# Load order, high-half casts and sample gating in a hybrid attention and recurrence layer

## The chip, the cores and the metric

The kernel runs on one core of a Trainium2 chip as one launch. The metric is the device time of an execution in microseconds (us), measured several times; beside the times there is one execution recorded by the profiler, from which all durations come. Engines: PE (TensorE; PEld is its loading of weights), DVE (VectorE), ACT (ScalarE), POOL (GpSimd) and SP (SyncE), which in this kernel issues every transfer (DMA).

## The reference

One step of a one-layer encoder, for a prompt of 2048 tokens and for 8 running samples of 16 new tokens each:

```python
proj = jnp.einsum('btd,de->bte', x, w_in)                 # D = 1024 -> 8 sections of 512
qa, ka, va, ga, qh, fh, ih, gh = jnp.split(proj, idx, axis=-1)

# A) stick-breaking attention, 8 heads x 64; samples see 1024 cached keys and values as well
z = jnp.einsum('bhqd,bhkd->bhqk', qblk, kf) * scale
log_keep = jnp.where(mask, jax.nn.log_sigmoid(-z), 0.0)
later = lax.cumsum(log_keep, axis=3, reverse=True) - log_keep
w = jnp.where(mask, jnp.exp(jax.nn.log_sigmoid(z) + later), 0.0)
o_sb = jnp.einsum('bhqk,bhkd->bhqd', w, vf) * jax.nn.silu(ga)

# B) HGRN2 recurrence, 4 heads x 128, chunk by chunk: S_t = diag(f_t) S_{t-1} + k_t outer i_t, o_t = S_t^T q_t
o_hg = rms_norm(o_hg) * norm_g * jax.nn.silu(gh)

out = jnp.einsum('bte,ed->btd', jnp.concatenate([o_sb, o_hg], -1), w_out)
y = layer_norm(alpha * x + out, ln_g, ln_b)
```

The keys, values and the recurrence's last states are outputs too.

## The kernel before

Matrix products of the projections are made in three passes, with each factor split into a high half (rounded to a short form) and a low half (the rest): `split(hi_engine, lo_engine, ...)` writes both, the high one by the helper of line 109 (ACT, a cast) or 111 (POOL), the low one as a difference in line 117. The program has these stages, by the profile's times:

- 0 to about 1010 us: the input projection, in two halves of tokens, section by section in tiles of 384 or 256 tokens. `pe_T` (L309-315) and `pe_N` (L323-325) make the products, `evac_T` (L336-367) and `evac_N` take them out of PSUM. For queries and keys of the prompt `evac_T` copies with ACT into `ev` (L352), splits with POOL into `e2` (high half L111, low half L117) and stores to `qT_d` or `kT_d` in device memory (L362); of gates it makes a SiLU into `ev` (L333) and stores to `gT_d` (L358). The weights' low halves `wl` are POOL's too (L117). The recurrence of the heads (`hgrn`, L405-540) is woven in as chains: intra-chunk scores `ps` (L430-469) from `hq` and `kS` (DVE, L455-456), outputs `on` (DVE, L518) and `qz` (POOL, L532).
- about 1010 to 1600 us: attention of the prompt, in units of one query block by up to 512 keys. `z_part` makes scores z from `kst` and `qr` (L742, L744); the sigmoids are ACT's (L747, L750); `s_part` scans the products of what is kept (DVE, L711) and multiplies them into the weights s (POOL, L764); `t_part` transposes these to wt (PE, L777); `c_part` multiplies with the values `vst` (L795); `finish` gates by `gt` into `mo` and stores a pair of blocks to `mx_d` (L800-815).
- woven into it until about 1353 us, as a guest whose pieces are taken at a set rate: the samples. `sample_init` (L818-842) makes the new tokens' own scores, sends them through device memory (`zn_d`, L836) and reads them back as `snc` (eight loads, L841), after which POOL masks them (L842). Then come rounds, two per sample (keys 512 to 1023, then 0 to 511): `sample_k` transposes cached keys `kr` (L877) and makes scores, `sample_r` scans, `sample_v` turns the weights and multiplies with cached values `vr` (36 matmuls, L958, in four runs with other work between), `sample_o` copies the result to `om` (ACT, L969), transposes it to `pse` (L973) and gates it into `ms_` (DVE, L978). `pk`, `zs`, `so` and `pse` share two PSUM buffers, in turn.
- until 1749 us: the output projection and the LayerNorm, the second guest.

What sets the order: the attention advances in steps of two halves. `at(step, fn)` puts loads at a step (L719-730; a step before the first is taken as the first, that is -12, before the attention itself). `later` holds work for the next half step. `defer(fn, n)` puts a transfer at the end of one list; each `tick()`, once in a half step, counts all entries down and issues from the front those that have come to zero, so that an entry is never issued ahead of one put there earlier. All transfers are then issued by SP, in the order of the program: one that waits for its data or its buffer holds all behind it. `load_k`, `load_v` and `load_q` (L170-193) fetch keys, values and queries of the prompt, `load_g` (L713) a gate, `load_ks` (L845) and `load_vs` (L853) cached keys (1 MB each, two buffers) and values (0.5 MB each, four buffers).

## Time and profile before

| | us |
|---|---|
| median of 3 runs | 1758.91 (1754.67 to 1759.86) |
| the profiled execution, whole | 1750.87 |
| its span, first to last instruction | 1749.1 |
| mean granted TensorE clock (1 is full speed) | 0.990 |

The page gives busy times of each engine; an engine's busy time is that of its instructions, without register, semaphore and transfer-issuing ones. A wait is the idle time of an engine just ahead of an instruction, put down to what released it last. In rows of groups stand the line, engine and operation, output<-input with shape, the count, then busy us and mean ns of one, then the idle time ahead and its releasers. In the rows of the timeline stand the start, the duration, the engine and line, and in brackets the idle time before with its releaser; xN means N instructions in one row. Buffer numbers are left out of names.

### The profile page before, as it was taken

Reading aid. Unit: us, or ns where it says so; the run is one execution under the profiler, and the core shown is the slowest. Engines: PE = TensorE matmul, PEld = TensorE weight load, DVE = VectorE, ACT = ScalarE, POOL = GpSimd, SP = SyncE. Lnnn points to the kernel's source line nnn. Section 1 sums busy time; section 2 is a strip of 40 time slices with the busy share of each in tenths; the row PEclk is TensorE's granted clock in tenths of the full one; section 3 lists DMA queues with packets and bytes.
Section 4 is the critical chain, followed back from the end, with each engine's and each line's share of the span. In section 5 each row is a group of like instructions: output and inputs, shape, how many; then the busy total and the mean of one; then the engine's idle time right before and its main releaser. Section 6 shows DMA issues by size and latency. Waiting matters only on the chain.

```text
span 1749.1 us, 33560 instructions
## 1 busy us (share of the span) xinstructions
PE 1673.7 (96%) x12901; PEld 1517.1 (87%) x12901; DVE 978.7 (56%) x1762; ACT 688.9 (39%) x1593; POOL 830.6 (47%) x918
## 2 busy tenths in 40 slices
PE   8999999999989999999999979999999999999998
PEld 8999999999979999999999957777777777778886
DVE  4264543255544263641746347787878786666554
ACT  3221220212213121221122147777878997775110
POOL 1252323232552151331324546676767876665664
PEclk9999999999999999999999988999999999999999
DMA  5133132122345133231212397989895764431443
GB/s 162 56 114 102 62 95 79 44 73 63 95 127 166 37 112 83 67 111 43 73 51 90 111 224 157 212 180 212 175 220 126 224 166 112 105 88 57 134 147 116
DMA packets 298792, 204.13 MB, mean 117 GB/s; under 512 B 113533, under 2 KB 275849, under 8 KB 298633
## 3 DMA queue, kind: packets, MB, share of 16 engines
q1 hardware_dynamic: 298632, 201.98, 43.9%
q8 instruction: 103, 1.69, 0.4%
q14 instruction: 57, 0.46, 0.1%
HBM read 146.36 MB, written 56.10 MB: 116 GB/s over the span
## 4 chain that ended last, share of the span: by engine, by line
PE 82%; DVE 6%; ACT 4%; DMA 3%; issue 2%; POOL 1%; SPq 1%; POOLq 0%; DVEq 0%; ACTq 0%
PE pj L313 10%; PE pj L315 10%; PE pj L314 10%; PE po L795 7%; PE z L742 5%; PE wt L777 5%; PE pj L323 4%; PE ps L430 4%; PE py L1125 4%; PE pj L325 4%; PE pj L324 4%; PE py L1127 4%; PE py L1126 4%; DMA qr<-qT_d 1%; DVE kS L456 1%
## 5 line engine op out<-in xcount | busy, mean ns | idle before, releaser
L313 PE MATMUL pj<-xh,wh 128*128 128x384 f32 (+1 forms) x1152 | 396.1, 344 | 0.0
L764 POOL TENSOR_TENSOR s<-s,pr 128x512 f32<-128x512 f32 (+3 forms) x320 | 324.9, 1022 | 121.8 <-DVE pr L711 103.8
L315 PE MATMUL pj<-xh,wl 128*128 128x384 f32 (+1 forms) x1152 | 376.6, 327 | 0.0
L314 PE MATMUL pj<-xl,wh 128*128 128x384 f32 (+1 forms) x1152 | 376.3, 327 | 0.0
L117 POOL TENSOR_TENSOR wl<-wr,wh 128x512 fp32r<-128x512 f32 x126 | 164.8, 1331 | 383.6 <-ACT wh L109 383.5
L711 DVE TENSOR_TENSOR_SCAN pr<-keep,pr,one 128x513 f32<-128x513 f32 x192 | 238.4, 1270 | 47.8 <-ACT keep L750 36.7
L313 PEld LDWEIGHTS pj<-xh,wh 128*128 128x128 f32 x1152 | 217.9, 189 | 2.7 <-issue 0.7
L314 PEld LDWEIGHTS pj<-xl,wh 128*128 128x128 f32 x1152 | 218.1, 189 | 0.7 <-issue 0.7
L315 PEld LDWEIGHTS pj<-xh,wl 128*128 128x128 f32 x1152 | 217.3, 189 | 0.0
L742 PE MATMUL z<-kst,qr 128*128 128x512 f32 (+3 forms) x640 | 186.2, 401 | 21.5 <-DMA qr<-qT_d 12.6
L109 ACT COPY wh<-wt 128x512 f32<-128x512 f32 (+3 forms) x320 | 165.0, 548 | 87.4 <-PE wt L777 85.8
L747 ACT ACTIVATE s<-z 128x512 f32<-128x512 f32 (+3 forms) x320 | 183.1, 572 | 19.4 <-PE z L744 15.6
L777 PE MATMUL wt<-ident,s 128*128 128x128 f32 x1088 | 166.3, 281 | 2.1 <-POOL s L764 1.9
L323 PE MATMUL pj<-wh,xh 128*128 128x256 f32 x544 | 160.6, 295 | 0.0
L777 PEld LDWEIGHTS wt<-ident,s 128*128 128x128 f32 x1088 | 123.8, 142 | 35.9 <-issue 16.3
L324 PE MATMUL pj<-wl,xh 128*128 128x256 f32 x544 | 152.6, 281 | 0.1
L325 PE MATMUL pj<-wh,xl 128*128 128x256 f32 x544 | 152.5, 280 | 0.0
L742 PEld LDWEIGHTS z<-kst,qr 128*128 128x128 f32 x640 | 105.1, 195 | 43.5 <-ACT keep L750 18.8
L795 PEld LDWEIGHTS po<-wh,vst 128*64 128x64 f32 x2176 | 118.0, 137 | 26.2 <-issue 18.0
L111 POOL TENSOR_SCALAR e<-ev 128x384 fp32r<-128x384 f32 (+1 forms) x48 | 53.1, 1106 | 178.6 <-ACT ev L352 159.2
L795 PE MATMUL po<-wh,vst 128*64 128x128 f32 x2176 | 137.3, 277 | 0.0
L750 ACT ACTIVATE keep<-z 128x512 f32<-128x512 f32 (+2 forms) x230 | 133.7, 581 | 0.0
(164 smaller groups left out, 2936.5 us busy)
## 6 DMA issues: line engine op xcount, KB each, us to landing
wr<-in_w_in SPq DMA_DIRECT2D x64, 512.0 KB
qr<-qT_d SPq DMA_DIRECT2D x64, 256.0 KB
kr<-in_cache_k SPq DMA_DIRECT2D x16, 1024.0 KB
vr<-in_cache_v SPq DMA_DIRECT2D x32, 512.0 KB
kst<-kT_d SPq DMA_DIRECT2D x24, 512.0 KB
mt<-mx_d SPq DMA_DIRECT2D x136, 64.0 KB
x<-in_x_prompt SPq DMA_DIRECT2D x16, 512.0 KB
out<-xr SPq DMA_DIRECT2D x16, 512.0 KB
```

Of the source, the lines that this page charges most:

```text
L313: mm(o, wh[:, k], xh[:, k, :n], start=k == 0, stop=False)
L314: mm(o, wh[:, k], xl[:, k, :n], start=False, stop=False)
L315: mm(o, wl[:, k], xh[:, k, :n], start=False, stop=k == KT - 1)
L323: mm(o, xh[:, k, ts], wh[:, k], start=k == 0, stop=False)
L324: mm(o, xh[:, k, ts], wl[:, k], start=False, stop=False)
L325: mm(o, xl[:, k, ts], wh[:, k], start=False, stop=k == KT - 1)
L711: dve.tensor_tensor_scan(pr[:, CW - wd:CW + 1][:, ::-1], kr, by, carry, ALU.mult, ALU.bypass)
L742: mm(z[:, :wd], q[:, a, r, q0:q0 + P], k[:, a, k0:k0 + wd], start=r == 0, stop=r == 1 and not top)
L747: act.activation(s[:, :wd], z[:, :wd], AF.Sigmoid, scale=SC)
L764: pool.tensor_tensor(s[:, :wd], s[:, :wd], pr[:, CW - wd + 1:CW + 1], ALU.mult)
L777: nc.tensor.transpose(pt_[:, x:x + P], U[(u, a)][0][:, x:x + P], ident)
L795: mm(o[r], v[:, lo // P % 8 + x, r], th[a][:, x * P:(x + 1) * P], start=top and x == 0, stop=bot and x == n - 1, skip_group_check=True)
```

## The change

Four things are edited.

1. `evac_T`: the high half of prompt queries and keys is made by ACT instead of POOL (48 tiles, 32 of 384 tokens and 16 of 256), `e2` has two buffers instead of one, `ev` two instead of three, and the store is deferred four ticks instead of three.
2. Loads of the first attention job (the loop of L719-730): the second query group is loaded at the very start instead of four steps before its use; the second pieces of keys and values and the gates, which were loaded at the start, come at steps of their own.
3. Stores of `mo` are deferred six ticks instead of four. `load_ks` in `sample_k` is deferred two ticks. `sample_v` makes its 36 matmuls in one run and then defers all four loads of the next sample's values by three ticks, where it issued each load between the runs.
4. `sample_o` keeps the copies `om` of four samples (five buffers) and then makes the four transposes into one PSUM tile and the gate in eight DVE instructions, where every sample had one transpose and two. At the end eight ticks instead of four empty the list.

```diff
             elif sec == GH:
                 silu_to(hg["g"][:, t0:t0 + n], o, n, ng[:, j:j + 1])
             else:
-                e = ev.tile([P, TW], F32, name="ev", tag="ev", bufs=3)
+                e = ev.tile([P, TW], F32, name="ev", tag="ev", bufs=2)
                 if sec == GA:
                     silu_to(e[:, :n], o, n)
                 else:
                     act.copy(e[:, :n], o)
                 if sec != GA:
-                    e2 = ev.tile([P, 2, TW], F32R, name="e2", tag="e2", bufs=1)
+                    e2 = ev.tile([P, 2, TW], F32R, name="e2", tag="e2", bufs=2)
                 for a, c, m in spans(half, t0, n):
                     if sec == GA or c == T:
                         d = gT_d[j][:, c:c + m] if sec == GA else (qn_d if sec == QA else kn_d)[j]
                         defer(lambda d=d, a=a, m=m: dma.dma_start(d, e[:, a:a + m]))
                         continue
-                    split(pool, pool, e2[:, 0, :m], e2[:, 1, :m], e[:, :m])
+                    split(act, pool, e2[:, 0, :m], e2[:, 1, :m], e[:, :m])
                     d = (qT_d if sec == QA else kT_d)[j]
                     defer(lambda d=d, c=c, m=m: dma.dma_start(d[:, :, c:c + m].rearrange("s p t -> p s t"),
-                                                              f32(e2[:, :, :m])), 3)
+                                                              f32(e2[:, :, :m])), 4)
                 if sec == KA:
                     return (half, j, t0, n, e)
...
             order_c = list(chunks(job))[::1 if b0 == 0 else -1]
             for i, c in enumerate(order_c):
                 if job or c:
-                    at((n0 - 5, n0 + 1 if b0 == 0 else n0 - 2)[i] if job else -99, lambda j=job, c=c: load_k(j, c))
-                at((n0, first[job] + (3 if b0 == 0 else 0))[i] if job else -99, lambda j=job, c=c: load_v(j, c))
+                    at((n0 - 5, n0 + 1 if b0 == 0 else n0 - 2)[i], lambda j=job, c=c: load_k(j, c))
+                at((n0 if job else -99, first[job] + (3 if b0 == 0 else 0))[i], lambda j=job, c=c: load_v(j, c))
             for g in range(b0 // 4, b1 // 4):
                 n1 = first[(p, g)] - LZ
                 if job or g:
-                    at(n1 - 4, lambda p=p, g=g: load_q(p, g))
-                at(n1 + GO if job else -99, lambda p=p, g=g: load_g(p, g))
+                    at(n1 - 4 if job or g > 1 else -99, lambda p=p, g=g: load_q(p, g))
+                at(n1 + GO, lambda p=p, g=g: load_g(p, g))
         def z_part(u):
             if u >= NU or u < 0:
...
                 done.add((p, qb // 2))
             if e:
-                defer(store, 4)
+                defer(store, 6)
         def sample_init():
...
                 pool.memset(sn, 0.0)
                 pool.tensor_copy(sn[:, cs], snc[:, b])
                 rows[b] = sn
-            load_ks(*((b, 0) if c == 1 else (b + 1, 1)))
+            defer(lambda: load_ks(*((b, 0) if c == 1 else (b + 1, 1))), 2)
             kr = kraws.pop((b, c))
             ks_ = []
             for p in range(4):
...
                 for p in range(4):
                     r = slice(32 * p, 32 * p + 32)
                     mm(o[r], t[:, r], v(p), start=n == 0, stop=n == len(blocks) - 1)
-                if n in (2, 4, 6):
-                    if b + 1 < NB:
-                        load_vs(b + 1, 1 if n < 6 else 0, (n // 2 - 1) % 2)
-                    yield
             if b + 1 < NB:
-                load_vs(b + 1, 0, 1)
-            yield
+                for c in (1, 0):
+                    for jh in range(2):
+                        defer(lambda c=c, jh=jh: load_vs(b + 1, c, jh), 3)
+            yield
+
+        oms = []
         def sample_o(b):
-            om = sk.tile([P, P], F32, name="om", tag="om")
+            om = sk.tile([P, P], F32, name="om", tag="om", bufs=5)
             act.copy(om, so.pop(b))
-            yield
-            yield
-            pse = px.tile([P, 4, 2, TS], F32, name="pse", tag="px")
-            nc.tensor.transpose(pse.rearrange("q p a t -> q (p a t)"), om, ident)
+            oms.append(om)
+            if len(oms) < 4:
+                return
+            yield
+            yield
+            b0 = b - 3
+            pse = px.tile([P, 4, 4, 2, TS], F32, name="pse", tag="px")
+            for i in range(4):
+                nc.tensor.transpose(pse[:, i].rearrange("q p a t -> q (p a t)"), oms[i], ident)
+            oms.clear()
             def gate():
                 for a in range(2):
                     r = slice(a * DH, (a + 1) * DH)
-                    dve.tensor_tensor(ms_[r, :, b * TS:(b + 1) * TS], pse[r, :, a],
-                                      gs[r, :, b * TS:(b + 1) * TS], ALU.mult)
+                    v = lambda t: t[r, :, b0 * TS:(b0 + 4) * TS].rearrange("d p (b t) -> d b p t", t=TS)
+                    for i in range(4):
+                        dve.tensor_tensor(v(ms_)[:, i], pse[r, i, :, a], v(gs)[:, i], ALU.mult)
             later.append(gate)
             yield
...
         run_later()
         run_later()
         run_later()
-        for _ in range(4):
+        for _ in range(8):
             tick()
         for _ in guest:
             run_later()
```

How instructions stand. First SP's transfers from the first load of values in the attention on, before the change (`kst`, `vst`, `qr`, `gt`: keys, values, queries, gates of the prompt; `qs`, `ks`, `vs`, `gs`: the samples' new tokens; `kr`, `vr`: cached keys and values; `mx_d`: the store of `mo`):

```order
L185 DMA vst<-v_d 128x8x128
L178 DMA kst<-kT_d 64x2x512 x2
L185 DMA vst<-v_d 128x4x128
L716 DMA gt<-gT_d 128x512 x3
L192 DMA qr<-qT_d 64x2x512 x4
L819 DMA qs<-qn_d 128x4x128
L820 DMA ks<-kn_d 128x4x128
L850 DMA kr<-in_cache_k 128x32x64
L823 DMA vs<-vs_d 128x512
L824 DMA gs<-gT_d 128x4x128
L836 DMA zn_d<-ss 128x512 x2
L841 DMA snc<-zn_d 16x8x16 x8
```

The same queue from the same load on, after the change:

```order
L185 DMA vst<-v_d 128x8x128
L192 DMA qr<-qT_d 64x2x512 x4
L178 DMA kst<-kT_d 64x2x512 x2
L716 DMA gt<-gT_d 128x512
L819 DMA qs<-qn_d 128x4x128
L820 DMA ks<-kn_d 128x4x128
L716 DMA gt<-gT_d 128x512
L850 DMA kr<-in_cache_k 128x32x64
L823 DMA vs<-vs_d 128x512
L824 DMA gs<-gT_d 128x4x128
L185 DMA vst<-v_d 128x4x128
L836 DMA zn_d<-ss 128x512 x2
```

The second `qr` has moved from behind `kst`, `vst` and three `gt` to the place behind the first `vst`; of the three `gt` one has stayed ahead of the samples' loads, one has moved between them and one is further behind, and the second `vst` has moved back behind `gs`.

SP a little later, from the eight `snc` loads on, before:

```order
L841 DMA snc<-zn_d 16x8x16 x8
L855 DMA vr<-in_cache_v 128x8x128 x4
L811 DMA mx_d_79<-mo 128x256
L850 DMA kr<-in_cache_k 128x32x64
L192 DMA qr<-qT_d 64x2x512 x4
L811 DMA mx_d_79<-mo 128x256
```

And after:

```order
L841 DMA snc<-zn_d 16x8x16 x8
L855 DMA vr<-in_cache_v 128x8x128 x4
L192 DMA qr<-qT_d 64x2x512 x4
L811 DMA mx_d_79<-mo 128x256
L850 DMA kr<-in_cache_k 128x32x64
L811 DMA mx_d_79<-mo 128x256
```

The load of cached keys that followed the first `mx_d` store has gone behind the third `qr` and that store.

ACT in the projection, at the first section of keys (`pj` the product in PSUM, `ev` its copy, `e` the split, `kn` keys in natural order), the piece of the difference:

```order
 L352 COPY ev<-pj 128x384
+L109 CAST e_916<-ev 128x384
 L109 CAST wh<-wr 128x512 x2
 L109 CAST dh<-dp 128x384 x2
 L373 COPY kn<-kn 128x384
 L352 COPY ev<-pj 128x384
-L373 COPY kn<-kn 128x384
-L352 COPY ev<-pj 128x384
-L373 COPY kn<-kn 128x384
-L352 COPY ev<-pj 128x384
+L109 CAST e_987<-ev 128x384
```

Behind each copy of a product there is now the cast of its high half, ahead of the casts of weights `wh`.

PE among the samples' products, the piece of the difference (`so` the outputs of one sample, `vr` cached values, `wt` the transposes of the attention):

```order
 L958 MATMUL so<-vs,swN 32x128 x4
-L958 MATMUL so<-vr,swT 32x128 x8
+L958 MATMUL so<-vr,swT 32x128 x32
 L877 MATMUL pk<-ident,kr 128x128 x4
 L777 MATMUL wt<-ident,s 128x128 x4
```

The 32 matmuls with cached values stand in one piece, where eight were followed by the next keys' transposes and the other 24 came in three more pieces.

## The prediction

> **What bounds the kernel now.** I read the page's busy times first, then busy time by stage, then TensorE's waits.
>
> ```profile
> span 1749.1 us, 33560 instructions
> PE 1673.7 (96%) x12901; PEld 1517.1 (87%) x12901; DVE 978.7 (56%) x1762; ACT 688.9 (39%) x1593; POOL 830.6 (47%) x918
> ```
>
> PE is busy for 96% of the span. The change adds and removes none of its work, so only its idle time, 75 us at most, and stretches at a low clock can be won. By stage (core time, PE, PEld, DVE, ACT, POOL busy, then clock, DMA share, GB/s):
>
> ```profile
> 0.00:1000.00 1000.00, 971.15 (x6937) 944.83 (x6938) 465.35 (x1141) 216.90 (x548) 334.80 (x365) 1.00 0.29 87
> 1000.00:1075.00 75.00, 58.20 (x406) 48.43 (x406) 35.24 (x46) 37.72 (x89) 35.33 (x58) 0.82 0.87 194
> 1075.00:1350.00 275.00, 262.42 (x2835) 212.41 (x2831) 221.11 (x273) 213.37 (x495) 199.22 (x252) 1.00 0.88 190
> ```
>
> The poor stage is the start of attention: 16.8 of 75 us idle, clock 0.82, DMA engines 87% busy. The samples' stage (1075 to 1350) has 12.6 idle in 275. TensorE's waits, totals with counts and the longest:
>
> ```profile
> PE z L742 <- DMA qr<-qT_d: 12.6, 4, 8.0
> PE ps L430 <- DVE kS L456: 8.6, 8, 1.8
> PE pk L877 <- ACT om L969: 6.0, 6, 1.4
> PE pk L877 <- DVE ms__10334 L978: 5.2, 6, 1.4
> ```
>
> These are what the change can reach: query loads at the start, recurrence chains that wait for VectorE, the gating of the samples' outputs.
>
> **Part 1, the start of attention.** On PE, then on SP's queue, which issues every transfer in order (times of issue, bracketed the idle time before):
>
> ```profile
> 1012.12 0.41 PE L742 MATMUL z<-kst,qr 128*128 128x128 f32 x2 [2.71 <-DMA qr<-qT_d]
> 1026.59 0.66 PE L742 MATMUL z<-kst,qr 128*128 128x128 f32 x2 [7.98 <-DMA qr<-qT_d]
> 1043.45 0.44 PE L777 MATMUL wt<-ident,s 128*128 128x128 f32 x2 [1.72 <-POOL s L764]
> 1057.88 0.97 PE L877 MATMUL pk<-ident,kr 128*128 128x128 f32 x4 [2.11 <-DMA kr<-in_cache_k]
> 1061.41 0.66 PE L742 MATMUL z<-kst,qr 128*128 128x128 f32 x2 [1.70 <-DMA qr<-qT_d]
> ```
> ```profile
> 1004.54 6.14 SPq L358 DMA_DIRECT2D gT_d<-ev  x3
> 1012.04 1.24 SPq L178 DMA_DIRECT2D kst<-kT_d  x2
> 1013.32 0.60 SPq L185 DMA_DIRECT2D vst<-v_d  x1
> 1013.97 1.45 SPq L716 DMA_DIRECT2D gt<-gT_d  x3
> 1015.52 4.22 SPq L192 DMA_DIRECT2D qr<-qT_d  x4
> 1034.35 0.89 SPq L836 DMA_DIRECT2D zn_d<-ss  x2
> 1037.20 3.77 SPq L841 DMA_DIRECT2D snc<-zn_d  x8
> ```
>
> The 8 us stall: two kst pieces (0.52 MB), a vst (0.26) and three gt (0.79), 1.57 MB by their tile sizes, are issued ahead of the second qr; at 194 GB/s that is 8.1 us. The change puts this qr ahead of all but the first vst. I take 2 us for what stays of 7.98 (its own 1.05 MB takes 5.4), so −6.
>
> Three things give it back. First, `ev` has two buffers now: the third gate tile of the last section needs the buffer whose store (the L358 rows) stands behind the 2 MB of first kst and qr. Its store, and every load behind it, goes out about 2 us later, and the first z too, at about 1013.5: +1.4. Second, of the same bytes all but one gt (0.26 MB, 1.3 us) still move before zn_d and the eight snc loads, for which POOL waits:
>
> ```profile
> POOL snc L842 <- DMA snc<-zn_d: 5.6, 1, 5.6
> ```
>
> Behind that wait POOL's multiplication s (L764) is queued, and behind s the PE row at 1043.45. The stage moves as many bytes as the DMA engines deliver (0.87 busy), so a new order changes which consumer waits. I put this point at +0.7 against before, late loads (2) less the gt not sent (1.3): the −4.6 won up to there is given back. Third, the samples' key load is deferred two ticks and now stands behind the third qr (1.05 MB, 5.4 us). The row at 1057.88 waits 2.11 already; kr comes at about 1062 (1057.9 + 5.4 − 1.3). What PE does between 1057.88 and 1059.71, where its wait for qr begins at the row of 1061.41, then ends at 1063.8, 2.4 late; I take 0.9 off for matmuls ahead of kr that find their qr now. Up to there PE idles some 6 us in one piece. After idle pieces like that it is slow:
>
> ```profile
> 1065.58 2.05 PE L742 MATMUL z<-kst,qr 128*128 128x512 f32 x4
> 1071.32 1.17 PE L742 MATMUL z<-kst,qr 128*128 128x512 f32 x4
> ```
>
> The same four matmuls take 2.05 and 1.17. Net for the start: **+1.5**, from −8 (all of 12.6 but the first 2.71 and some 2 of remainder) to +3.7 (kr 5.4 later in full, with nothing filled in).
>
> A sentence beside those two rows: the Trainium skill, page "TensorE: Matmul & The Clock Gate", section "Part 1: The HAM clock gate", has the array at half rate after an idle window of about 3.4 us until as long has been busy; the trace agrees (0.82 here, 2.05 against 1.17), and by the rule one idle piece of 6 would cost about 2 us more than pieces of 2.1 and 1.7, which is an estimate from that page and lies inside my range.
>
> **Part 2, the high halves go from POOL to ACT in the projection.** 48 instructions move. POOL's, and the nearest ACT casts of those sizes (total us, mean ns):
>
> ```profile
> L111 POOL TENSOR_SCALAR e<-ev 128x384 fp32r<-128x384 f32 x32 | 39.2, 1224 | 133.5 <-ACT ev L352 129.4 <-issue 4.0
> L109 ACT CAST dh<-dp 128x384 fp32r<-128x384 f32 x20 | 9.5, 513 | 0.0
> ```
>
> POOL's following work can begin 1.22 − 0.51 = 0.7 earlier where it was waiting for ACT's copy, up to 1.2 where POOL lags; ACT has 48 × 0.5 = 24 us more on 217 busy in 1000. PE gains only where a stall ends on work behind POOL's. In the stage there are these:
>
> ```profile
> 261.57 0.68 PE L430 MATMUL ps<-hq,kS 128*128 128x128 f32 x4 [1.35 <-DVE kS L456]
> 495.22 0.91 PE L430 MATMUL ps<-hq,kS 128*128 128x128 f32 x6 [1.38 <-DVE kS L456]
> 770.90 0.35 PE L430 MATMUL ps<-hq,kS 128*128 128x128 f32 x1 [1.83 <-DVE kS L456]
> 517.25 0.55 PE L522 MATMUL pq<-ident,on 128*128 128x128 f32 x3 [2.05 <-DVE on L518]
> 523.70 0.70 PE L537 MATMUL pb<-qz,kN 128*128 128x512 f32 x1 [3.28 <-POOL qz L532]
> 993.85 0.33 PE L522 MATMUL pq<-ident,on 128*128 128x128 f32 x1 [1.69 <-DVE on L518]
> ```
>
> Three kS stalls × 0.8, on 0.75, qz 0.7 and on 0.95 make −4.8; about 0.3 is lost where a cast delays one of ACT's evacuations. So **−4.5**. Bounds: −7 (all six lose 1.2) to +2 (no stall shortens, and four of the casts hold up an evacuation by 0.5). POOL's part in kS needs its own look, first POOL, then DVE:
>
> ```profile
> 256.34 1.18 POOL L111 TENSOR_SCALAR e<-ev 128x384 fp32r<-128x384 f32 x1 [12.08 <-ACT ev L352]
> 258.57 5.23 POOL L117 TENSOR_TENSOR wl<-wr,wh 128x512 fp32r<-128x512 f32 x4
> ```
> ```profile
> 256.98 0.35 DVE L456 TENSOR_TENSOR kS<-kS,tot 128x192 f32<-128x192 f32 x1
> 260.01 1.42 DVE L456 TENSOR_TENSOR kS<-kS,tot 128x192 f32<-128x192 f32 x1
> ```
>
> kS takes 0.35 beside POOL's tensor_scalar and 1.42 beside its tensor_tensor. The change removes the first kind and keeps the second, which merely moves 0.7 to 1.2 earlier, partly out of kS's way: hence 0.8 of 1.07.
>
> The Trainium skill, page "SBUF — State Buffer", section "Who interferes with whom", says that a DVE instruction with two SBUF inputs contends with any GpSimd instruction that reads SBUF, so the removed copies too would have been blocking DVE; the row at 256.98 speaks against it for this form. By the rule the sum would be lower, a rival below.
>
> **Part 3, samples' outputs gated four batches at a time.** The 5.2 us of pk waiting for ms, in six pieces, become one wait at the first group of four, since pk takes its buffer from a gate of eight DVE instructions, 8 × 0.22 = 1.8, instead of two; the last gate has no pk behind it:
>
> ```profile
> L978 DVE TENSOR_TENSOR ms__10334<-pse,gs x16: 190/222/228, 1122.7 to 1352.8; 64x64 f32<-64x64 f32 x16
> ```
>
> So **−3** (bounds −1.5, if the eight overrun by as much again, to −4.5). The 6.0 for om stays: om is copied in every batch, and the next pk takes that buffer as before.
>
> **Part 4, deferred transfers and one run of products.** One run of 36 matmuls is the same PE work. What it removes is SP's waiting:
>
> ```profile
> SPq L855 <- PE so L958: 66.4, 19, 12.9
> ```
>
> The four loads now go out when the buffers are free. But no PE row waits for a vr, or for a kr after 1057.88, so this wins 0. The mixed store waits six half steps instead of four; it stands at the front of a first-in list, so what is deferred behind it (kr's load) waits too. kr has two buffers and a round is about 275 / 16 = 17 us: cover enough, I think. **0** (−2 to +3).
>
> **Sum.** +1.5 − 4.5 − 3 + 0 = −6 against the profiled execution's 1750.87, so 1744.9 for such an execution. That execution lies 8.0 under the median of 1758.91, which is what the result is compared with; the same −6 there gives **1752.9**, say 1753. The own range of this case, the bounds without the two ends that are rivals below (9.5 lower at the start, 6.5 higher in the projection), is 1747 to 1760.
>
> **Rivals.**
> *The stalls at the start really go.* For it: the 8 us stall has one visible cause. Against it: the snc chain. If snc is not last (POOL's 5.6 has some slack, or PE finds other work), −8 in place of +1.5: 1743.4. Chance 0.17.
> *DVE is freed everywhere* (the page's rule as a mechanism of this kernel: kS returns to 0.35 in all eight stalls). All 8.6 go instead of 3 × 0.8 = 2.4: 6.2 lower, 1746.7. Chance 0.08, against the row at 256.98.
> *Nothing reaches PE in the projection.* The stalls end on wl's tensor_tensor wherever it lies, or ACT's casts delay evacuations by as much: +4.5, so 1757.4. Chance 0.20. Here the change would not do what it says.
> *Slower: kr comes late at the heads of rounds.* Its load waits behind the mixed store in the list and behind four vr loads (2.1 MB, 11 us at 190 GB/s) in SP's queue. Against it: 17 us a round. Each such round costs the 2.11 of the row at 1057.88 and about 2 more at a low clock, the excess of two groups like 2.05 against 1.17: 4 us. Of 14 later rounds, two eat the forecast's gain and more make it slower; four make −6 + 15 = +9, 1768. Chance 0.15.
> The forecast has 0.40.
>
> **How the numbers follow.** A measurement tells 0.3% from no change, 5.3 us: below 1753.6 is faster, above 1764.2 slower. The forecast's own range lies on both sides of 1753.6: 0.22 of its 0.40 is faster. With 0.17 and 0.08 that makes faster 0.47. Same: 0.18 of the forecast and 0.18 of the third rival, 0.36. Slower: 0.15 and 0.02 of the third rival with the bounds' bad ends, 0.17. The range takes the first rival nearly whole, 1742, and half of the slower case, 1766; some 0.17 is left out. The likeliest result by itself is a gain on the edge of what can be told.
>
> **What would show it.** Right: the second z stall near 2, but PE at the L764 rows of about 1043 no earlier, and kr the longest wait about 1062; DVE's kS waits down from 8.6 by 2 to 3; one ms wait; none of PE for vr. Wrong: wt near 1043 comes 4 or more earlier (first rival); kS waits under 2 (second); kS, on and qz waits unchanged (third); several waits pk <- kr after 1075 (fourth), or any wait of PE for vr or for mx loads of the output projection, which I price at nothing.

## The result and the profile after

The changed kernel takes 1745.54 us (median of 7 runs, 1742.53 to 1747.60); beside it the kernel before takes 1754.67 (median of 7, 1751.17 to 1759.86; the three runs that were known before are among them). The ratio is 0.9941, 95% interval 0.9923 to 0.9959: faster by 0.6%, some 10 us (7 to 14 by the interval). The prediction said −6 us, which against its own median was 0.9966.

The profiled execution of the changed kernel, busy time by stage (core time, PE, PEld, DVE, ACT, POOL, then clock, DMA share, GB/s):

```profile
span 1745.2 us, 33561 instructions
0.00:1000.00 1000.00, 973.32 (x6946) 946.58 (x6947) 458.67 (x1141) 239.93 (x596) 283.06 (x319) 1.00 0.29 87
1000.00:1075.00 75.00, 56.86 (x419) 47.30 (x417) 36.36 (x47) 38.28 (x90) 34.83 (x56) 0.84 0.84 188
1075.00:1350.00 275.00, 265.35 (x2921) 218.95 (x2918) 224.62 (x280) 218.05 (x506) 202.80 (x254) 1.00 0.87 191
```

POOL lost 52 us in the projection (334.8 before) and ACT took 23 (216.9 before). The start of attention is as poor as it was: PE 56.9 busy of 75, the DMA engines 84% busy. TensorE's waits:

```profile
PE pk L877 <- DMA kr<-in_cache_k: 8.7, 2, 6.1
PE ps L430 <- DVE kS L456: 8.4, 9, 1.4
PE pk L877 <- ACT om L969: 6.1, 6, 1.4
PE z L742 <- DMA qr<-qT_d: 3.8, 2, 3.1
PE z L742 <- DMA kst<-kT_d: 3.1, 1, 3.1
```

The wait for queries went from 12.6 to 3.8, and one for cached keys (2.1 before) came up to 8.7; pk's waits for ms are not in the list any more. The same places of the timeline as before:

```profile
992.18 0.44 PE L522 MATMUL pq<-ident,on 128*128 128x128 f32 x2 [0.91 <-DVE on L518]
...
1021.52 0.41 PE L742 MATMUL z<-kst,qr 128*128 128x128 f32 x2 [3.07 <-DMA qr<-qT_d]
...
1042.71 0.44 PE L777 MATMUL wt<-ident,s 128*128 128x128 f32 x2 [1.60 <-POOL s L764]
1061.21 1.12 PE L877 MATMUL pk<-ident,kr 128*128 128x128 f32 x4 [6.13 <-DMA kr<-in_cache_k]
...
1113.76 0.63 PE L877 MATMUL pk<-ident,kr 128*128 128x128 f32 x4 [1.18 <-ACT om L969]
...
1344.01 0.33 PE L978 MATMUL pse<-ident,om 128*128 128x128 f32 x1 [1.55 <-ACT om L969]
```

Of before, two of these points have not been shown:

```profile
1115.31 0.66 PE L877 MATMUL pk<-ident,kr 128*128 128x128 f32 x4 [1.11 <-ACT om L969]
1352.24 0.33 PE L973 MATMUL pse<-ident,om 128*128 128x128 f32 x1 [0.43 <-ACT om L969]
```

Three rows of the same work cut each execution into four stretches: pq near 992, the first pk that waits for om (near 1114), the last pse (near 1344), and the end of the span. Every execution below is cut at its own rows, so that one stretch is compared without what was won or lost ahead of it:

| us | clock, 500 to 560 | to pq | pq to pk | pk to last pse | rest | span |
|---|---|---|---|---|---|---|
| before | 1.00 | 993.85 | 121.46 | 236.93 | 396.9 | 1749.1 |
| changed | 0.97 | 992.18 | 121.58 | 230.25 | 401.2 | 1745.2 |
| e1 cast and buffers | 0.94 | 992.19 | 123.46 | 237.18 | 395.6 | 1748.4 |
| e12 cast alone | 0.97 | 990.44 | 122.51 | 238.47 | 397.0 | 1748.4 |
| e2 loads | 0.94 | 996.35 | 120.89 | 236.95 | 397.5 | 1751.7 |
| e3 one run | 0.91 | 997.28 | 120.43 | 236.79 | 395.5 | 1750.0 |
| e4 gates | 0.94 | 996.34 | 122.30 | 230.94 | 396.0 | 1745.6 |
| e5 deferrals | 0.97 | 995.52 | 123.42 | 236.87 | 399.0 | 1754.8 |
| e6 changed, keys at once | 1.00 | 989.53 | 120.19 | 230.27 | 395.9 | 1735.9 |
| e7 changed, kst earlier | 0.97 | 990.78 | 121.80 | 230.22 | 398.5 | 1741.3 |
| e8 changed, old buffers | 1.00 | 989.48 | 117.74 | 230.24 | 396.6 | 1734.1 |
| e9 changed, e6 and e8 | 0.97 | 990.74 | 119.59 | 231.19 | 397.3 | 1738.8 |
| e10 e9, other deferrals out | 0.97 | 990.73 | 119.04 | 230.91 | 397.7 | 1738.4 |
| e11 e9, old order of loads | 1.00 | 988.95 | 119.74 | 230.31 | 397.4 | 1736.4 |

The first and the last column also move by 3 to 5 us between executions whose code there is the same (e2 to e5 and before in the first; e6, e8 and the changed kernel in the last), and pq to pk by some 2 (before, e3 and e4). In the first column the scatter goes with the granted TensorE clock between 500 and 560 us: the waits for on and qz near 517 and 522 are followed by pieces at a low clock in some executions and not in others, and each step down of this clock (1.00, 0.97, 0.94, 0.91) comes with 0.8 to 1.7 us more in the mean of the executions with, and of those without, the cast. The span of one execution therefore tells less than the ratios, and of a stretch only what several executions show is used. The changed kernel's own profile shows −1.7, +0.1, −6.7 and +4.3; the last is not in the others.

### The profile page after: what moved, and what is told of

It is laid out like the page before. It is cut to its first block, busy times and chain, and to the rows that moved or that the text cites. A ratio compares the mean times of both kernels' runs of the same rounds, so it can differ in the third digit from the quotient of the medians.

```text
span 1745.2 us, 33561 instructions
## 1 busy us (share of the span) xinstructions
PE 1672.4 (96%) x12901; PEld 1519.8 (87%) x12901; DVE 971.0 (56%) x1762; ACT 710.9 (41%) x1641; POOL 776.6 (44%) x870
## 4 chain that ended last, share of the span: by engine, by line
PE 81%; DVE 5%; ACT 4%; DMA 4%; issue 2%; POOL 2%; SPq 1%; POOLq 0%; DVEq 0%; ACTq 0%
PE pj L313 10%; PE pj L315 10%; PE pj L314 10%; PE po L795 6%; PE z L742 5%; PE wt L777 5%; PE ps L430 4%; PE pj L323 4%; PE pj L325 4%; PE pj L324 4%; PE py L1132 3%; PE py L1134 3%; PE py L1133 3%; PE pk L877 2%; DVE kS L456 2%
## 5 line engine op out<-in xcount | busy, mean ns | idle before, releaser
L742 PE MATMUL z<-kst,qr 128*128 128x512 f32 (+3 forms) x640 | 187.6, 404 | 17.9 <-ACT keep L750 6.3
L117 POOL TENSOR_TENSOR e<-ev,e 128x384 fp32r<-128x384 f32 (+1 forms) x48 | 45.3, 943 | 221.1 <-ACT e L109 152.4
```

Source lines behind the costliest of these rows:

```text
L117: eng_lo.tensor_tensor(lo, src, f32(hi), ALU.subtract)
L742: mm(z[:, :wd], q[:, a, r, q0:q0 + P], k[:, a, k0:k0 + wd], start=r == 0, stop=r == 1 and not top)
```

## The experiments

Each was timed in five rounds beside the kernel before; ratios are to that kernel, and 0.0010 is 1.75 us.

**Cast and buffers (e1).**

```diff
-                e = ev.tile([P, TW], F32, name="ev", tag="ev", bufs=3)
+                e = ev.tile([P, TW], F32, name="ev", tag="ev", bufs=2)
...
-                    e2 = ev.tile([P, 2, TW], F32R, name="e2", tag="e2", bufs=1)
+                    e2 = ev.tile([P, 2, TW], F32R, name="e2", tag="e2", bufs=2)
...
-                    split(pool, pool, e2[:, 0, :m], e2[:, 1, :m], e[:, :m])
+                    split(act, pool, e2[:, 0, :m], e2[:, 1, :m], e[:, :m])
...
-                                                              f32(e2[:, :, :m])), 3)
+                                                              f32(e2[:, :, :m])), 4)
```

> The kernel before with the first edit alone: high halves cast by ACT, two ev and two e2 buffers, the store deferred four ticks. Theory (the whole change is a sum of four independent terms, sized by the two traces): -3.7 us, ratio 0.998; the stalls of ps for kS that end at about 262, 495 and 771 shorter by 0.6 to 0.8 each, those of pq for on and of pb for qz by 0.7 to 0.8 each, and two of the kS stalls of the later chains longer by 0.5 to 1.2, so that the kS total stays above 8. The prediction had -4.5 with the kS total falling to about 6. Rival (the Trainium skill, page SBUF - State Buffer, section Who interferes with whom: every POOL instruction that reads SBUF blocks a DVE instruction with two SBUF inputs; as a mechanism here: 48 fewer blockers): DVE's kS instructions get shorter in the mean and the kS waits sum to under 2, -8 us or more. Rival two: the cast delays ACT's evacuations by as much, 0 us.

Measured: 0.9985 (0.9972 to 0.9997), −2.6 us. The first gate tile of the last section now holds up the third (before, this instruction waited 2.20 for ACT). In e1 it waits 5.67; these are the changed kernel's row of DVE and, behind it, the second z of the attention on PE:

```profile
1011.70 0.42 DVE L333 TENSOR_TENSOR ev<-pj,sg 128x256 f32<-128x256 f32 x1 [5.66 <-DMA gT_d<-ev]
```
```profile
1012.18 0.69 PE L742 MATMUL z<-kst,qr 128*128 128x128 f32 x2 [1.84 <-DVE ev L333]
```

Counted from pq, this second z stands at 20.0 in e1 and in the changed kernel, at 18.6 in e12 and at 17.9 in e8, which have three `ev` buffers. So it comes 1.4 and 2.1 later with two, and by the row it waits for DVE's gate itself, not for a load.

**Cast alone (e12).**

```diff
-                    split(pool, pool, e2[:, 0, :m], e2[:, 1, :m], e[:, :m])
+                    split(act, pool, e2[:, 0, :m], e2[:, 1, :m], e[:, :m])
```

> The kernel before with one word changed: the high halves cast by ACT, the projection's buffers and the deferral as before. Theory: the first edit is a gain by the cast and a loss by the third ev buffer taken away; the first edit alone gave 0.9985, the changed kernel with the buffers given back gained 0.0016 to it, so the cast by itself is worth 2.6 + 2.8 = 5.4 us or, by its stalls, the predicted 4.5: 0.997 to 0.9975. In its trace the start of attention comes no later against the projection's end than before. Rival: the buffers matter only beside the new order of loads, and the cast alone gives 0.9985 again.

Measured: 0.9973 (0.9959 to 0.9987), −4.7 us. To pq, the five executions without the cast take 993.85 to 997.28 (mean 995.9), the nine with it in the table 988.95 to 992.19 (mean 990.6): −5.3. At equal clock between 500 and 560 us, it is 993.85 against a mean of 989.3 (clock 1.00), 995.52 against 991.0 (0.97) and 996.35 against 992.19 (0.94): −4.2 to −4.6. So the cast is worth what was forecast. What e1 changes beside it (the two buffer counts and the deferral, not taken apart) is 0.9985 against 0.9973, +2.1; the two intervals overlap, so by the ratios alone this loss is not told from nothing. TensorE's stalls in e12:

```profile
PE ps L430 <- DVE kS L456: 8.4, 9, 1.4
```

and in the changed kernel, one after the other:

```profile
495.25 0.91 PE L430 MATMUL ps<-hq,kS 128*128 128x128 f32 x6 [0.70 <-DVE kS L456]
516.52 0.55 PE L522 MATMUL pq<-ident,on 128*128 128x128 f32 x3 [1.26 <-DVE on L518]
522.21 2.08 PE L537 MATMUL pb<-qz,kN 128*128 128x512 f32 x2 [2.53 <-POOL qz L532]
770.33 0.68 PE L430 MATMUL ps<-hq,kS 128*128 128x128 f32 x4 [1.16 <-DVE kS L456]
773.31 0.68 PE L430 MATMUL ps<-hq,kS 128*128 128x128 f32 x4 [1.23 <-DVE kS L456]
```

1.38, 2.05, 3.28 and 1.83 have become 0.70, 1.26, 2.53 and 1.16, each shorter by 0.7 to 0.8, and so has the 1.35 of 261.57 (0.70). The stall at 773.31 is new, another near 975 grew from 0.47 to 1.00, and that is why the kS total is 8.4 and not 6: PE comes earlier to a chain where kS still lies beside POOL's tensor_tensor. The new stall costs next to nothing. Before, PE came late to this chain because its granted clock was 0.66 between 770 and 775 us, behind the stall of 1.83; here it is 1.00. From the ps row at 770 to the ps row at 775 it is 4.65 us before and 4.57 here. DVE's kS group over the first 1000 us, first of before, then of e1 (count, total us, mean ns):

```profile
L456 DVE TENSOR_TENSOR kS<-kS,tot 128x192 f32<-128x192 f32 x108 | 66.8, 619 | 0.0
```
```profile
L456 DVE TENSOR_TENSOR kS<-kS,tot 128x192 f32<-128x192 f32 x108 | 65.6, 608 | 0.0
```

With 48 POOL instructions fewer that read SBUF, the mean falls by 11 ns, where the rival needed the long ones gone. In the timeline of before, the 128x192 kS that lie beside a POOL tensor_tensor take 1.22 us in the mean (32 of them), those that lie nearly wholly beside its tensor_scalar 0.42 (19), those beside neither 0.38 (68). By the rule of the Trainium skill (page "SBUF — State Buffer", section "Who interferes with whom") all POOL instructions that read SBUF contend with such an instruction; for POOL's tensor_scalar in this form the runs do not bear it out.

**The loads of the first job (e2).** The four `at(...)` lines of the change, nothing else.

> The kernel before with the second edit alone: the first attention job's loads in the new order, nothing else. Theory: the stage's transfers are bound by what the DMA engines deliver, so the 8 us stall for the second qr shrinks to about 3 and the time is given back at the POOL multiplication that waits for snc near 1043: between -1 and 0 us at the third stall (1043.45 before), and since the key load is not deferred here, no 6 us stall for kr near 1060, so the total is -2 to 0 us. The prediction had +1.5 for the start with the deferred key load. Rival: the stall really goes, -6 to -8 us (ratio 0.996).

Measured: 0.9993 (0.9984 to 1.0002), −1.2 us, not told from nothing. PE's stall for the second qr fell from 7.98 to 3.02, and POOL's wait behind it rose:

```profile
1023.92 0.41 PE L742 MATMUL z<-kst,qr 128*128 128x128 f32 x2 [3.02 <-DMA qr<-qT_d]
...
1044.96 0.44 PE L777 MATMUL wt<-ident,s 128*128 128x128 f32 x2 [1.59 <-POOL s L764]
```
```profile
POOL snc L842 <- DMA snc<-zn_d: 9.4, 1, 9.4
```

5.6 became 9.4, and PE waits 2.39 for the first cached keys where it did not before. From pq to the wt row it is 49.6 us before and 48.6 here, and to the first pk that waits for om 121.5 and 120.9. Five of the 8 us were taken away at one place; 1.0 was left of them at the wt row and 0.6 at pk.

**One run of products (e3).**

```diff
-                if n in (2, 4, 6):
-                    if b + 1 < NB:
-                        load_vs(b + 1, 1 if n < 6 else 0, (n // 2 - 1) % 2)
-                    yield
             if b + 1 < NB:
-                load_vs(b + 1, 0, 1)
+                for c in (1, 0):
+                    for jh in range(2):
+                        load_vs(b + 1, c, jh)
             yield
```

> The kernel before with the samples' 36 value matmuls in one run, the four loads issued at its end with no deferral. Theory: TensorE loses about 0.14 us each time it goes from these 32-column matmuls to another kind and back; 3 breaks fewer in each of 8 batches make -3.4 us (0.998), seen in the so group as busy time 17.5 to 13.5 and issue idle 4.5 to 1.3. The prediction had 0 for it. Rival: the gain of the samples' stage came from the transfers that no longer block the queue, then this alone gives 0, or is slower by some us because four loads wait in SP's queue for one another's buffers.

Measured: 0.9986 (0.9975 to 0.9998), −2.4 us. Here is what a break costs. Before, a piece of 16 (eight products, two entries each), three times with what follows:

```profile
1141.97 0.64 PE L958 MATMUL so<-vr,swT 128*32 128x128 f32 x16
1142.55 0.55 PE L777 MATMUL wt<-ident,s 128*128 128x128 f32 x3
1143.02 0.65 PE L958 MATMUL so<-vr,swT 128*32 128x128 f32 x16
1143.48 1.04 PE L885 MATMUL zs<-kt,qbd 128*32 128x512 f32 x8
...
1147.32 0.64 PE L958 MATMUL so<-vr,swT 128*32 128x128 f32 x16
1147.90 1.09 PE L777 MATMUL wt<-ident,s 128*128 128x128 f32 x8
```

In the changed kernel, all in one:

```profile
1136.15 1.93 PE L958 MATMUL so<-vr,swT 128*32 128x128 f32 x64
1138.01 0.66 PE L877 MATMUL pk<-ident,kr 128*128 128x128 f32 x4
```

Read from start to start: the piece ahead of zs, which has the same tile of 128 rows by 32 columns, takes 0.46; the two ahead of a 128 by 128 matmul take 0.58. A change of tile costs 0.12. The four pieces of a sample take 2.17 (the first, ahead of pk, 0.55), the 64 in one piece 1.86 with one such change at their end: 0.31 a sample, 2.5 in eight. The Trainium skill, page "TensorEngine Tiling (Array Packing)", section "Key Properties", says that changing the tiling mode drains the TensorE; these rows agree. PE's busy time between pk and the last pse falls by as much, from 225.2 to 222.8 in e3, and from 224.4 in e4 to 221.9 in the changed kernel. But the stretch itself hardly gets shorter (236.79 against 236.93, 230.25 against 230.94): idle time grows instead. Of e3's 2.2 us more, 1.5 is at the last pse (L971 there), which waits 1.9 for om where L973 waited 0.4 before. The ratio's interval reaches from −0.4 to −4.4 us, so how much of the 2.5 arrives is not settled.

**Four batches gated together (e4).** The diff's piece of `sample_o`, nothing else.

> The kernel before with the outputs of four batches transposed and gated together. Theory: the six waits of pk for ms (5.2 us) go altogether, since the gate runs while pk's buffer is not yet wanted, and the last transpose waits 1.2 longer for om: -4.0 us (0.9977). The prediction had -3, with one wait of 1.8 left in the middle. Rival: pk then waits as long for another holder of the two PSUM buffers (om), 0 to -1 us.

Measured: 0.9965 (0.9953 to 0.9977), −6.1 us; its stretch is 6.0 shorter, and the changed kernel has the same. The first group of four in the changed kernel, on PE and on DVE:

```profile
1224.63 0.60 PE L877 MATMUL pk<-ident,kr 128*128 128x128 f32 x4
...
1226.05 0.66 PE L877 MATMUL pk<-ident,kr 128*128 128x128 f32 x4 [0.49 <-ACT kt L879]
```
```profile
1223.98 1.26 DVE L711 TENSOR_TENSOR_SCAN spr<-skp,spr,one 128x513 f32<-128x513 f32 x1
1225.15 1.25 DVE L986 TENSOR_TENSOR ms__10328<-pse,gs 64x64 f32<-64x64 f32 x8
```

And one of the gates before, of which eight were made; six had a pk waiting behind them:

```profile
1157.23 1.25 DVE L711 TENSOR_TENSOR_SCAN spr<-skp,spr,one 128x513 f32<-128x513 f32 x1
1158.41 0.43 DVE L978 TENSOR_TENSOR ms__10334<-pse,gs 64x64 f32<-64x64 f32 x2
```

The gate's own work was 0.43; what PE waited for was its place behind DVE's scan, in all six cases. The eight instructions of a group take 1.25 (0.16 each from start to start, where 0.22 was forecast), and no pk waits for them: the 0.49 at 1226.05 is put down to ACT's copy kt of the pk ahead, and this pk starts before the eight have ended (1226.4). So where a wait of 1.8 was forecast there is none for ms. Why pk is no longer held by the gate was not looked into. Of the 6.0 that the stretch lost, 5.2 is idle time and 0.75 PE's busy time; no run explains the second part.

**The deferrals (e5).** Products still in four pieces, the end's ticks eight.

```diff
-                defer(store, 4)
+                defer(store, 6)
...
-            load_ks(*((b, 0) if c == 1 else (b + 1, 1)))
+            defer(lambda: load_ks(*((b, 0) if c == 1 else (b + 1, 1))), 2)
...
-                        load_vs(b + 1, 1 if n < 6 else 0, (n // 2 - 1) % 2)
+                        defer(lambda n=n: load_vs(b + 1, 1 if n < 6 else 0, (n // 2 - 1) % 2), 3)
...
-                load_vs(b + 1, 0, 1)
+                defer(lambda: load_vs(b + 1, 0, 1), 3)
```

> The kernel before with the deferred transfers alone: stores of mo six ticks, the samples' key load two, each value load three ticks after the point where it stood, products still in four pieces. Theory: no wait of TensorE in the samples' stage ends on a transfer, so nothing is won there; the first deferred key load goes behind the third qr and the stall that ends near 1058 before grows from 2.1 to about 6: 0 to +2 us in the time. The prediction had 0 for the rest and +1.5 for the start, most of it from this. Rival (SP's blocked queue costs time): the samples' stage gets shorter by 2 us or more, ratio 0.9985 or less.

Measured: 1.0015 (1.0001 to 1.0028), +2.6 us for the three deferrals together. The key load stands behind the third qr:

```profile
1065.63 1.12 PE L877 MATMUL pk<-ident,kr 128*128 128x128 f32 x4 [8.51 <-DMA kr<-in_cache_k]
```

SP waits 20.2 us for so where it waited 66.4, and the samples' stretch is 236.87, as before (236.93): that waiting cost PE nothing.

**The changed kernel with the keys at once (e6).**

```diff
-            defer(lambda: load_ks(*((b, 0) if c == 1 else (b + 1, 1))), 2)
+            load_ks(*((b, 0) if c == 1 else (b + 1, 1)))
```

> The changed kernel with the samples' key load issued at once again, all else as changed. Theory: the 6.1 us stall for kr near 1061 shrinks to 2 to 3 and a wait of 2 for the third qr comes behind it instead: -0.5 to -2 us against the changed kernel (0.9941 of before becomes 0.993 to 0.994). Rival: the stall is a whole loss and goes whole, -4 us and the low clock after it with it (0.9915).

Measured: 0.9922 (0.9904 to 0.9940) against 0.9941 (0.9923 to 0.9959), −3.3 us, between theory and rival; the intervals overlap. The row near 1061 is now:

```profile
1053.75 0.66 PE L877 MATMUL pk<-ident,kr 128*128 128x128 f32 x4 [3.29 <-DMA kr<-in_cache_k]
1057.05 0.66 PE L742 MATMUL z<-kst,qr 128*128 128x128 f32 x2 [2.20 <-DMA qr<-qT_d]
```

**The changed kernel with kst a step earlier (e7).**

```diff
-                    at((n0 - 5, n0 + 1 if b0 == 0 else n0 - 2)[i], lambda j=job, c=c: load_k(j, c))
+                    at((n0 - 5, n0 + 1 if b0 == 0 else n0 - 3)[i], lambda j=job, c=c: load_k(j, c))
```

> The changed kernel with the second key piece of the second pass's jobs fetched one step earlier (n0 - 3). Theory: in the profile of the changed kernel 4.4 us of the 8.2 won by 1350 are lost by 1400, in a wait for kst (3.1 where 1.4 was) and a low clock behind it, because this load stands behind the output projection's first loads; one step earlier it stands ahead of them, the wait at about 1366 is under 1 and the loss goes: -2 to -4 us against the changed kernel, 0.992 to 0.993 of before. Rival: the loss is one of that execution alone (the clock), 0 to -1 us.

Measured: 0.9944 (0.9927 to 0.9961), no gain. e6, e7 and e8 were timed in the same rounds: e7, by its ratio as fast as the changed kernel, has a median of 1744.37 us (1742.12 to 1746.81), e6 1740.02 (1737.78 to 1742.42), e8 1741.37 (1736.26 to 1743.33). The kst wait of 3.1 is gone and a new one stands ahead of it:

```profile
1357.49 0.50 PE L1132 MATMUL py<-woh,mh 128*128 128x512 f32 x1 [2.47 <-ACT mh L109]
```

The output projection's first loads now come behind kst. My theory here fell: the 4 us that the changed kernel's profile lost after 1344 are that execution's; e6 and e8, with the same code there, do not lose them. The rival was right.

**The changed kernel with the old buffers (e8).** The cast is still ACT's.

```diff
-                e = ev.tile([P, TW], F32, name="ev", tag="ev", bufs=2)
+                e = ev.tile([P, TW], F32, name="ev", tag="ev", bufs=3)
...
-                    e2 = ev.tile([P, 2, TW], F32R, name="e2", tag="e2", bufs=2)
+                    e2 = ev.tile([P, 2, TW], F32R, name="e2", tag="e2", bufs=1)
...
-                                                              f32(e2[:, :, :m])), 4)
+                                                              f32(e2[:, :, :m])), 3)
```

> The changed kernel with the buffers of the projection as before (three ev, one e2, the store deferred three ticks), the casts still ACT's. Theory: with three ev buffers the last gate tile does not wait for the store of the first one, and the start of attention comes 1.8 us earlier against the projection's end (the loss that the first edit alone showed there: from -1.07 at 950 to +0.71 at 1000 in its trace against before); with one e2 the casts wait for stores at some tiles, which costs 0 to 2 us in the projection: -1.5 to 0 us against the changed kernel. Rival: the start waits for the DMA engines and not for this tile, and one e2 holds ACT up, 0 to +3 us.

Measured: 0.9925 (0.9907 to 0.9943) against 0.9941, −2.8 us, more than expected, with intervals that overlap; from pq to pk 117.74 against 121.58 in the changed kernel and 121.80 in e7.

**Both repairs (e9), then without the other deferrals (e10), then with the old loads (e11).** e9 is the changed kernel with the edits of e6 and e8; e11 is e9 with the four `at(...)` lines as before; e10 is e9 with four ticks at the end again and

```diff
-                defer(store, 6)
+                defer(store, 4)
...
-                        defer(lambda c=c, jh=jh: load_vs(b + 1, c, jh), 3)
+                        load_vs(b + 1, c, jh)
```

> The changed kernel with both findings: the samples' key load issued at once, and the projection's buffers as before (three ev, one e2, deferral three), casts still ACT's. Theory: the two repairs are at different transfers and add: 0.9922 and 0.9925 against 0.9941 make 0.9906 (1738 where before is 1754), and in its trace the start of attention (the kr row near 1055) waits under 4 in one piece. Rival: both repair the same thing, the supply of the start by the DMA engines, and only one counts: 0.992.

> The one before in this call without the two deferrals left: mo stored after four ticks, value loads issued right behind the run of products. Theory: no TensorE wait ends on these, so the same as that one within 0.1%: 0.990 to 0.992. Rival (they do clear the queue for something): slower than it by 2 us or more.

> The first of this call with the first attention job's loads in the old order. Theory: the order gives back at the snc wait what it wins at the second qr, so the new order is worth 0 to 1.2 us (0.9993 alone): 0.991 to 0.992 here. Rival: with the other two out of the way the stall's 5 us count, and without the new order this is 4 us or more slower than the first.

Measured: e9 0.9902 (0.9887 to 0.9918), 1737.65 us; e10 0.9917 (0.9905 to 0.9929); e11 0.9922 (0.9910 to 0.9935). e9 is faster than the changed kernel by 0.4%, with intervals apart, and has the lowest ratio of all. The forecast for two repairs that add was 0.9906, and the 0.992 of the rival, where only one counts, lies just outside e9's interval. e10 and e11 are a little slower than e9, but the intervals overlap, and in the traces neither stretch shows it: e11, with the old order of loads, takes 119.74 from pq to pk, e9 119.59, e10 119.04. Whether the new load order and the other deferrals are worth 0 or 3 us is left open.

## Why the prediction was right, and where its steps were off

The direction was right, faster, and 1745.54 lies within the range of 1742 to 1766. It does not lie within the forecast's own range of 1747 to 1760: the lower end of the wide range was set by the first rival, which the runs refute, so that the number fell inside is in part luck. Of the 7.4 between the forecast 1752.9 and the measured time, 4.2 is the median of before, which moved from 1758.91 to 1754.67 with more runs; the rest is that the change is worth more than −6. The forecast's mechanism held in the projection and in most of the start; the size fell short in two terms, the gates and the one run (ratios as us of 1754.7).

| step | predicted | measured | by |
|---|---|---|---|
| cast in the projection | −4.5 | −4.7 | e12 |
| start: buffers | +1.4 at the first z | +2.1 to +3.5 | e1 less e12, e8, e9 less e6 |
| | | +1.4 to +2.1 at the second z | rows of e1 and e12, changed and e8 |
| start: load order | −4.6, given back by 1043 | −1.2 | e2 |
| start: deferred keys | kr 4 later, the rest of +1.5 | +2.6 to +4.0 | e5 (all deferrals), e6, e9 less e8 |
| start, whole | +1.5 | +0.1 to +0.3 | stretch pq to pk |
| gates | −3 | −6.1 | e4 |
| one run | 0 | −2.4 | e3 |
| sum of the parts | −6 | −9.7 | e1 to e5 |
| whole | −6 | −10.4 | ratio |

- **Start, the rows.** Each of the three losses was found in its row: DVE's third gate tile waits 5.66 for a store, POOL's snc wait went from 5.6 to 9.6 in the changed kernel, kr stands at 1061 where 1062 was forecast. The path of the first was another: the first z is not late, the second waits for DVE's gate. The first rival, that the stall of 8 really goes, fell with e2.
- **Start, the sum.** The losses of buffers and of deferred keys rest on three comparisons of ratios each. All have the same sign, but the intervals overlap, or, for e5, hardly leave out no change (1.0001); only both together (e9) are clear. In the stretch from pq to pk, e9 is 1.9 longer than e8, against the other two comparisons for the keys. By the ratios the two losses sum to some 5 us, yet in the changed kernel this stretch is no more than 0.3 longer than before. One part of the reason stands in the rows behind kr. Counted from pq, kr comes 5.0 later in the changed kernel than before (69.0 against 64.0), but the next zs (L885) only 0.45 later. In all four executions with the key load deferred (changed, e5, e7, e8) it is 10.1 to 10.5 us from this kr row to that zs, in the ten others 13.3 to 15.3. So a late kr gives most of its loss back: the wait for the third qr behind it is gone, and the low clock ends sooner. The scatter of the stretch is some 2 us, so the net of +0.1 to +0.3 and the forecast's +1.5 are not told apart.
- **Start, the clock.** The estimate that one idle piece of 6 costs about 2 us more than pieces of 2.1 and 1.7 failed; it came out the other way. Before, the granted clock is 0.50 from 1058 to 1068, behind the wait of 2.11 and over that of 1.70; in the changed kernel, with one wait of 6.13, from 1058 to 1064, and only the last 3 us of that find PE at work. The four matmuls z that the prediction shows with 2.05 at 1065.58, slow behind the two shorter pieces, take 1.17 at 1065.59 in the changed kernel.
- **Projection.** The terms were right one by one (0.65 to 0.8 each) and in the sum (−4.2 to −4.7). "kS waits down from 8.6 by 2 to 3" was wrong as a sign, since new kS stalls come up (773.31) when others shrink. The third rival, nothing reaches PE, fell with e12; the second, DVE freed everywhere, with the kS means.
- **Gates.** The step that failed is the "one wait at the first group of four", priced at "8 × 0.22 = 1.8". There is no wait for ms at all; the eight run in 1.25, and only 0.49 for ACT's copy is new. With the 5.2 gone whole, the term came to −6.1, beyond its bound of −4.5; the ratio's interval is −4.0 to −8.2.
- **One run.** The step that failed is "One run of 36 matmuls is the same PE work". It is the same count, but not the same time: each change of tile costs 0.12, PE is busy 2.4 us less in e3, and I had not looked at the rows from start to start. With it falls "The change adds and removes none of its work" as a bound on what can be won.
- **Deferrals.** "This wins 0" held for what they were to clear, and their loss was in the sum, at the start. The fourth rival (keys late at the heads of rounds) did not come: the only long kr waits lie ahead of 1075.

## What to carry to other kernels

Where the transfer engines are nearly full (0.87 busy here), a new order of loads moves the stall to the next consumer; look up what stands behind the promoted load before counting its stall as won. A small operation on a busy engine costs its place in the queue and not its duration, so asking four times less often is worth more than its own time says. Matmuls of one tile shape belong side by side. One execution's span is no measure of a change of 0.3%: look first for stretches in which the granted clock differs between executions of the same code.

## What the runs showed of the hardware

From a 128 by 32 matmul tile to a 128 by 128 one TensorE loses 0.12 us more (0.58 against 0.46 for the same piece) than from one use of the 128 by 32 tile to the next. Eight DVE multiplications of 64 by 64 from PSUM take 1.25 us one behind the other, 0.16 each, where single ones are listed with 0.22. DVE's kS (128x192, two inputs in SBUF) takes 0.42 us in the mean nearly wholly beside POOL's tensor_scalar and 1.22 beside its tensor_tensor. The granted TensorE clock fell to 0.50 at 1058 behind a wait of 2.11 (before). Between 500 and 560 us, where PE waits 1.3 to 3.3 near 517 and 522, its mean was 1.00 in four of the fourteen executions and 0.91 to 0.97 in ten.
